# Cosine and sine tables of a Fourier mixer: split on the chip, or stored as high and low parts and fetched by GpSimd's queue

## The chip, the cores and the metric

One core of one Trainium2 chip runs the whole program. The metric is the device time of one execution in microseconds (us). The kernel before has a median of 1548.53 us over three runs (1547.23 to 1550.25).

## The reference, cut to what matters

The program is a two-layer transformer block on 512 image tokens and 256 context tokens of width 1024. Layer 0 mixes with Fourier transforms, layer 1 with attention. The change lies in layer 0's mixer, which runs for the image tokens (x) and for the context tokens (c):

```python
def _fourier_hyena_mixer(h, w_in, w_out, conv_w, conv_b, ...):
    proj = h @ w_in
    u_f = _f32(proj[..., :D_FOURIER]).reshape(B, L, N_FOURIER_GROUPS, FOURIER_GROUP_DIM)
    y_f = jnp.fft.fft2(u_f, axes=(1, 3), norm='ortho').real.reshape(B, L, D_FOURIER).astype(h.dtype)
    u_h = _dwconv3(proj[..., D_FOURIER:], conv_w, conv_b)
    x0, x1, v = jnp.split(u_h, 3, axis=-1)
    spectrum = _hyena_filter_spectrum(L, w1, b1, w2, b2, w3, b3, w4, freq)
    y_h = x0 * _long_conv(v * x1, spectrum, hy_bias)
    return jnp.concatenate([y_f, y_h], axis=-1) @ w_out
```

All of it is float32. The transforms are products with tables of cosines and sines, which depend on no input.

## The kernel before, in words

**Products in three parts.** A float32 matrix is kept as a high part and a low part, each in the matmul's own rounded format (F32R). A product is three matmuls, high by high, high by low and low by high (`mm3`, L266 to L269). To make the parts of a weight or a table, SyncE loads the raw float32 tile (`wraw`, L253, tile `wr`), ScalarE copies it into the rounded format (`hi`, L240 to L244, tile `wh`), and VectorE subtracts the copy from the raw tile (`lo`, L247, tile `wl`). The pool `W` holds three buffers each of `wr`, `wh` and `wl`, of 128 x 1024 float32 (512 KB) each. A buffer is free again when its last reader has finished.

**Order.** The steps of the mixer's second half stand in a written order, `MIX_ORDER`. It fixes the order among these steps on TensorE, VectorE, ScalarE and GpSimd, each of which takes its instructions in turn and stands still where one waits. The loads on SyncE's queue, and instructions of the code behind (the modulation sums `junk` of L368 and the splits of the first w_out tiles), are placed between them by the framework's scheduler.

**The steps**, by the names in `MIX_ORDER`; a digit at the end is the tile:
- R, WH, WL: load, high part and low part of a tile in `W`. The tiles are w_in 6 and 7, the four tables u0, u1 (`utab`) and i0, i1 (`itab`), and w_out 0 (o0). u0 and u1 take the long convolution to frequencies, i0 and i1 bring it back.
- P11, P60 to P63, P70 to P73: the last products with w_in. CA, CB, CC: their short convolution, on ScalarE and VectorE.
- HP: the pool of the normed input (hh, hl) is closed. Its memory goes to yh, yl and to the tables cs, ct and st: `cs128` (128 x 256), `fcos` (128 x 1040) and `fsin` (128 x 1024).
- TH and TL: high and low part of these three, in pieces c0, c1, n0, n1 and s0.
- FM, FD, T3, UH, UL: product, fold and transposition of the last piece of the convolution's input.
- SC, SX: to frequencies, context and image (tables u0 for SC0, SC1, SX0, SX1, and u1 for SX2, SX3). D, Q, Y, L with A or B: product with the filter's spectrum on VectorE (D), on GpSimd (Q), then high part (Y, ScalarE) and low part (L, VectorE for A, GpSimd for B).
- IC, IX: back from frequencies, context with i0, image with i0 and i1; E, S, M, H, L behind them: unfold, multiply by x0, split.
- FH, FL: parts of a Fourier group, in `W`. FA, GA: first transform with cs (image, context); PH, PL, GH, GL: parts of the result; FB, GB: second transform with ct and st; FE, FS, GE, GS: unfold. ZH, ZL: parts for the last product.
- OA, OB0 to OB3: the first tile of the product with w_out. The other seven follow in `res_proj`.

The products of P, SC, SX, FA, GA, FB, GB and O use three PSUM buffers in turn, IC and IX two others.

The loads and splits of the tables go through these lines:

```python
def wraw(self, src, n=1024):
    raw = self.t(self.W, [P, 1024], F32, "wr")
    self.nc.sync.dma_start(raw[:, :n], src)
    return raw
...
def TH(n):
    o, m = chunk(n)
    self.hi(k_[tabs[n[0]][2] + "h"][:, o : o + m], k_["raw" + n][:, :m])

def TL(n):
    (o, m), t_ = chunk(n), tabs[n[0]][2]
    self.lo(k_[t_ + "l"][:, o : o + m], k_["raw" + n][:, :m], k_[t_ + "h"][:, o : o + m])
```

Of the kernel before, what the change touches and what calls it, by code (L numbers as in the profile page):

```python
# [12 lines left out]
F32R = mybir.dt.float32r  # L13
# [7 lines left out]
P = 128  # L21
# [74 lines left out]
KAx3 G3 KBx3 SDAx2 RG4 SQx2 G4 SDAx0 SPBx2 KAx2 SPBx0 SDBx2 SQx0 KBx2 SDBx0  # L96
"""
MIX_ORDER = """
P11 R6 R7 WH6 WL6 P60 CA11 P61 CB11 CC11 P62 FM Ru0 WH7 FD T3 P63 WHu0 UH CA6 WL7 UL WLu0 CB6 SC0 Ru1 CC6 DBc0 SC1 DAc1 QBc0 YBc0 LBc0 WHu1 Ri0 Rn1
P70 QAc1 YAc1 WLu1 P71 DAc0 P72 QAc0 P73 YAc0 WHi0 SX0 LAc1 DBc1 HP QBc1 Rs0 LAc0 WLi0 SX1 CA7 YBc1 THn1 LBc1 CB7 DBx0 IC0 QBx0 DAx0 TLn1 IC1 QAx0 FH0  # L100
Rc0 THc0 ICE0 THs0 YBx0 ICE1 YAx0 Rn0 ICS0 CC7 LBx0 IC2 FL0 ICS1 TLs0 Rc1 IC3 THn0 LAx0 GA0 DAx1 DBx1 QAx1 SX2 GH0 QBx1 FA0 GL0 TLc0 THc1 YAx1 YBx1
LBx1 LAx1 FH1 TLn0 TLc1 DAx2 DBx2 SX3 PH0 GB0 ICM0 FH2 QAx2 QBx2 PL0 YAx2 ICH0 YBx2 LAx2 FL1 DAx3 GE0 ICE2 LBx2 DBx3 ICL0 FL2 FB0 FA1 FE0 GS0 PH1 QAx3
Ri1 GA1 QBx3 FS0 ICM1 PL1 YBx3 ICH1 FA2 WHi1 ICL1 ICE3 FB1 ICS2 LBx3 WLi1 GH1 YAx3 PH2 GL1 GA2 LAx3 Ro0 FE1 IX1 PL2 GB1 ICS3 ICM2 IXE1 IX0 IXS1 FH3
FS1 ICH2 ICM3 GH2 ICH3 ICL2 IXM1 IXH1 IXE0 ICL3 IX2 GE1 IXS0 FB2 FL3 GS1 IXE2 IXM0 GL2 FA3 FE2 IXH0 IXS2 IX3 IXM2 IXH2 FS2 GA3 PH3 IXL1 IXL0 PL3 IXL2
IXE3 IXS3 GB2 WHo0 IXM3 IXH3 FB3 GH3 GE2 FE3 WLo0 GL3 GB3 GE3 ZH0 IXL3 GS2 FS3 GS3 OA ZL0 OB0 ZH1 ZL1 ZH2 ZH3 OB1 ZL2 ZL3 OB2 OB3
"""


# [80 lines left out]
class Builder:  # L189
# [380 lines left out]
    def mixer(self):  # L570
        nc, I = self.nc, self.I
# [18 lines left out]
        x = [self.t(xp, [P, TW], F32, f"x{d}") for d in range(KD)]  # L590
        hh, hl = [], []
# [5 lines left out]
        with self.tc.manual_schedule(engines={ENG.PE, ENG.DVE, ENG.SP, ENG.Activation}):  # L597
# [30 lines left out]
            h = layer(0, layer(0, pa, 1), 2)  # L628
# [18 lines left out]
            def both(d, step):  # L647
                a1(d, step)
                return a2(d, step)
# [24 lines left out]
            h = layer(1, layer(1, pa, 1), 2)  # L674
# [45 lines left out]
        def conv(m, dst, ps):  # L720
            c = m - 4
            self.conv3(dst, ps, self.col("hcw0", c), self.col("hcw1", c), self.col("hcw2", c), self.col("hcb", c), TW)
# [230 lines left out]
        k_ = {}  # L953
        wt = {}
        pl = {}
        src = {"6": I["w_in"][6], "7": I["w_in"][7], "o0": I["w_out"][0], **{f"u{a}": I["utab"][a] for a in range(2)}, **{f"i{a}": I["itab"][a] for a in range(2)}}
        sx = lambda: self.t(pl["Sx"], [P, 512], F32, "sx")
        es = lambda: self.t(pl["Sx"], [P, 260], F32, "e", 4)
        tabs = {"s": ("cs128", 256, "cs"), "c": ("fcos", 1040, "ct"), "n": ("fsin", 1024, "st")}

        def R(n):
            if n in src:
                k_["raw" + n] = self.wraw(src[n])
            else:
                o, m = chunk(n)
                k_["raw" + n] = self.wraw(I[tabs[n[0]][0]][:, o : o + m], m)

        def chunk(n):
            o = 520 * int(n[1])
            return o, min(520, tabs[n[0]][1] - o)  # L970

        def WH(n):
            raw = k_["raw" + n]
            h, l = self.t(self.W, [P, 1024], F32R, "wh"), self.t(self.W, [P, 1024], F32R, "wl")
            self.hi(h, raw)
            wt[n] = h, l, raw

# [8 lines left out]
        def PP(m, q):  # L986
            if q == 0:
                k_[f"ps{m}"] = self.mm()
            for k in (2 * q, 2 * q + 1):
                self.proj_k(k_[f"ps{m}"], wt[str(m)], hh, hl, k)  # L990
# [53 lines left out]
        def SP(s, ft):  # L1044
            nt, kp, km = (1, 4, 5) if s == "c" else (2, 0, 2)
            th, tl, _ = wt[f"u{ft // 2}"]
            ps = k_[f"sp{s}{ft}"] = self.mm()
            even = ft < 2 if nt == 2 else ft == 0
            for c in range(2):
                k0 = kp if (c == 0) == even else km  # L1050
                for i in range(nt):
                    o = 512 * (ft % 2) + 256 * i + 128 * c
                    w = slice(o, o + 128)
                    self.mm3(ps[:, 512 * c : 512 * c + 512], th[:, w], tl[:, w], uTh[:, k0 + i, :], uTl[:, k0 + i, :], i == 0, i == nt - 1)
# [64 lines left out]


        def TH(n):
            o, m = chunk(n)
            self.hi(k_[tabs[n[0]][2] + "h"][:, o : o + m], k_["raw" + n][:, :m])

        def TL(n):
            (o, m), t_ = chunk(n), tabs[n[0]][2]
            self.lo(k_[t_ + "l"][:, o : o + m], k_["raw" + n][:, :m], k_[t_ + "h"][:, o : o + m])

        def FH(g):
            k_[f"fu{g}"] = [self.t(self.W, [P, 1024], F32R, t_)[:, :TW] for t_ in ("wh", "wl")]  # L1130
# [63 lines left out]
        def O(ks):  # L1194
            if 4 in ks:
                k_["o"] = self.mm()
            h, l, _ = wt["o0"]
            for k in ks:
                w = slice(128 * k, 128 * k + 128)
                self.mm3(k_["o"][:, 0:512], h[:, w], l[:, w], yh[k][:, 0:512], yl[k][:, 0:512], k == 4, k == 3)  # L1200

        def step(s):
            if s[0] == "R":
                R(s[1:])
            elif s[:2] in ("WH", "WL"):
                (WH if s[1] == "H" else WL)(s[2:])
            elif s in ("P11", "FM", "FD", "T3", "UH", "UL", "HP"):
                {"HP": HP, "P11": P11, "FM": FM, "FD": FD, "T3": T3, "UH": UH, "UL": UL}[s]()
            elif s[0] == "P" and s[1] in "67":
                PP(int(s[1]), int(s[2]))  # L1210
            elif s[0] == "C":
                conv(int(s[2:]), s[1])
            elif s[:2] in ("SC", "SX"):
                SP(s[1].lower(), int(s[2]))
            elif s[1] in "AB" and s[0] in "DQYL" and len(s) == 4:
                {"D": DD, "Q": QQ, "Y": YY, "L": LL}[s[0]]("AB".index(s[1]), s[2], int(s[3]))
            elif s[:2] in ("IC", "IX"):
                {"": inv, "E": IE, "S": IS, "M": IM, "H": IH, "L": IL}[s[2:-1]](s[1].lower(), int(s[-1]))
            elif s[:2] in ("TH", "TL"):
                (TH if s[1] == "H" else TL)(s[2:])  # L1220
            elif s in ("OA", "OB0", "OB1", "OB2", "OB3"):
                O(range(4, KD) if s == "OA" else [int(s[2])])
            elif s[0] == "Z":
                (ZH if s[1] == "H" else ZL)(int(s[2]))
            elif s[0] == "F" and s[1] in "HL":
                (FH if s[1] == "H" else FL)(int(s[2]))
            elif s[0] == "P":
                (F1H if s[1] == "H" else F1L)(0, int(s[2]))
            elif s[:2] in ("GH", "GL"):
                (F1H if s[1] == "H" else F1L)(4, int(s[2]))  # L1230
            else:
                {"A": F1, "B": F2, "E": F2E, "S": F2S}[s[1]](0 if s[0] == "F" else 4, int(s[2]))
# [1341 lines left out]
def _f(a):  # L2574
    return np.ascontiguousarray(a, dtype=np.float32)
# [5 lines left out]
    return o  # L2581


def constants():
    f32 = np.float32
    c = {}
# [32 lines left out]
    ut = np.zeros((4, P, 2, 2, P))  # L2619
    it = np.zeros((4, P, 2, C))  # L2620
# [5 lines left out]
        it[a, :, 0, :] = np.cos(ac).T  # L2626
        it[a, :, 1, :] = np.sin(asn).T
    it[0, 0] *= 0.5
    c["utab"] = ut.reshape(2, 2, P, 512).transpose(0, 2, 1, 3).reshape(2, P, 1024)
    c["itab"] = it.reshape(2, 2, P, 512).transpose(0, 2, 1, 3).reshape(2, P, 1024)  # L2630
    k = np.arange(258)
    ang = TWO_PI * ((t[:, None] * k[None, :]) % T) / T
    fc = np.zeros((T, 260))
    fc[:, :258] = np.cos(ang)
    c["fcos"] = fc.reshape(4, P, 260).transpose(1, 0, 2).reshape(P, 1040)
    sn = np.sin(ang[:, :256])
    c["fsin"] = sn.reshape(4, P, 256).transpose(1, 0, 2).reshape(P, 1024)
    m = np.arange(P)
    a8 = TWO_PI * ((m[:, None] * m[None, :]) % P) / P
    c["cs128"] = np.concatenate([np.cos(a8), np.sin(a8)], 1) / 256.0  # L2640
    rows, cols = np.repeat(np.arange(8), 64).astype(f32), np.tile(np.arange(64), 8).astype(f32)
    inv = (f32(10000.0) ** (-np.arange(8, dtype=f32) / f32(8))).astype(f32)
    co, si = np.zeros((32, T)), np.zeros((32, T))
# [103 lines left out]
def arrays_of(inputs):  # L2747
    a = layouts(**{k: np.asarray(v) for k, v in inputs.items()})
    a.update(constants())
    return {k: np.ascontiguousarray(v) for k, v in a.items()}  # L2750
# [16 lines left out]
```

## Time and profile before

| | |
|---|---|
| median of 3 runs | 1548.53 us (1547.23 to 1550.25) |
| profiled execution, its own time | 1556.88 us |
| span of its instructions | 1555.0 us |
| TensorE busy in the span | 1505.8 us, 97% |
| VectorE busy | 1262.1 us, 81% |
| ScalarE busy | 740.6 us, 48% |
| GpSimd busy | 250.8 us, 16% |
| loads of SyncE's and the hardware queue | 162.73 MB |
| loads of GpSimd's queue | 60.91 MB |

In the profile PE is TensorE, PEld its weight load, DVE VectorE, ACT ScalarE, POOL GpSimd, and SP SyncE; a q behind a name means the queue that only issues. "L247" is a line of the kernel, and since `hi`, `lo` and `mm3` are helpers, many tiles share their lines; one goes by the tile names. "out<-in" names what is written and what is read. A row of waits says who waited for what, for how long in total, how often, and the longest. Matmuls overlap, so TensorE's busy time is not time at its peak rate.

### The profile page before, as it was taken

The page shows a single profiled execution, that of the slowest core. Times are in us where ns is not written, and L with a number is a line of the kernel's source. Part 1 is how long each engine was busy: PE and PEld are TensorE (multiplying, and loading weights), DVE is VectorE, ACT ScalarE, POOL GpSimd, SP SyncE. Part 2 cuts the span into 40 slices and gives each one's busy share as a digit, 9 for nine tenths or more (in the row PEclk, how much of TensorE's full clock was granted, in tenths as well). Part 3 has the DMA queues.
Part 4 walks back from the last instruction along what each step waited for, and adds up shares of the span by engine and source line. Part 5 has one row for each costly group of instructions (what it writes and reads, how often), then busy time and mean ns, then how long its engine had stood idle before and what let it go on. Part 6 is the DMA issues. An engine that isn't in the chain of part 4 may idle for free.

```text
span 1555.0 us, 24353 instructions
## 1 busy us (share of the span) xinstructions
PE 1505.8 (97%) x9352; PEld 1308.7 (84%) x9352; DVE 1262.1 (81%) x2084; ACT 740.6 (48%) x1126; POOL 250.8 (16%) x406
## 2 busy tenths in 40 slices
PE   7999998999999999999999999999999899999998
PEld 5687887888999999989998888766558899989997
DVE  5788969968997998777768776889956899878884
ACT  4451224426544443434434345898844655434442
POOL 0013125201112121112111000111211121112100
PEclk9999999999999999999999999999999999999999
DMA  9336522546267779768687731010124465656543
GB/s 350 118 109 203 186 69 68 172 134 211 63 174 191 188 182 212 186 178 217 174 233 189 271 85 44 4 41 28 35 90 131 107 175 152 165 139 157 144 112 104
DMA packets 87872, 225.19 MB, mean 145 GB/s; under 512 B 12843, under 2 KB 19213, under 8 KB 86733
## 3 DMA queue, kind: packets, MB, share of 16 engines
q1 hardware_dynamic: 63565, 162.73, 31.5%
q0 software_dynamic: 24192, 60.91, 18.9%
q8 instruction: 73, 1.20, 0.3%
q14 instruction: 42, 0.34, 0.1%
HBM read 201.96 MB, written 21.64 MB: 144 GB/s over the span
## 4 chain that ended last, share of the span: by engine, by line
PE 66%; DVE 16%; DMA 9%; issue 4%; ACT 3%; POOL 1%; SPq 0%; ACTq 0%; POOLq 0%; DVEq 0%
PE mm L267 15%; PE mm L268 15%; PE mm L269 15%; DVE junk L368 4%; DMA sb<-wmodT 3%; DVE wl L247 3%; PE pv L2128 3%; PE ms L267 2%; PE ms L269 2%; DMA sb<-w_up 2%; PE ms L268 2%; PE s L2076 1%; DMA sa<-w_up 1%; PE pv L2139 1%; ACT wh L242 1%
## 5 line engine op out<-in xcount | busy, mean ns | idle before, releaser
L242 ACT ACTIVATE wh<-wr 128x1024 fp32r<-128x1024 f32 (+3 forms) x179 | 155.0, 875 | 200.2 <-PE mm L268 121.3
L267 PE MATMUL mm<-hh,wh 128*128 128x512 f32 (+3 forms) x704 | 231.5, 329 | 1.1 <-DVE xr L1370 1.0
L269 PE MATMUL mm<-hh,wl 128*128 128x512 f32 (+3 forms) x704 | 229.1, 325 | 3.4 <-DVE wl L247 3.3
L268 PE MATMUL mm<-hl,wh 128*128 128x512 f32 (+3 forms) x704 | 229.4, 326 | 2.3 <-DVE hl L450 2.3
L247 DVE TENSOR_TENSOR wl<-wr,wh 128x1024 fp32r<-128x1024 f32 (+3 forms) x179 | 180.5, 1013 | 19.3 <-ACT wh L242 18.4
L267 PEld LDWEIGHTS mm<-hh,wh 128*128 128x128 f32 x704 | 133.9, 190 | 13.2 <-issue 3.7
L269 PEld LDWEIGHTS mm<-hh,wl 128*128 128x128 f32 x704 | 133.4, 190 | 13.5 <-DVE wl L247 5.8
L268 PEld LDWEIGHTS mm<-hl,wh 128*128 128x128 f32 x704 | 133.8, 190 | 11.2 <-DVE hl L450 3.3
L368 DVE SCALAR_TENSOR_TENSOR junk<-wr,sb 128x1024 bf16<-128x1024 f32 x96 | 117.1, 1220 | 6.0 <-DMA wr<-wmodT 6.0
L267 PE MATMUL ms<-hh,wh 128*128 128x386 f32 (+2 forms) x240 | 76.2, 317 | 1.1 <-DVE fg L1554 0.9
L269 PE MATMUL ms<-hh,wl 128*128 128x386 f32 (+2 forms) x240 | 76.3, 318 | 0.0
L268 PE MATMUL ms<-hl,wh 128*128 128x386 f32 (+2 forms) x240 | 76.2, 317 | 0.0
L269 PE MATMUL mm<-x,wl 128*128 128x512 f32 (+1 forms) x224 | 75.8, 338 | 0.3 <-DVE wl L247 0.3
L267 PE MATMUL mm<-x,wh 128*128 128x512 f32 (+1 forms) x224 | 76.0, 340 | 0.0
L268 PE MATMUL mm<-x,wh 128*128 128x512 f32 (+1 forms) x224 | 76.0, 339 | 0.0
L267 PE MATMUL mm<-ah,wh 128*128 128x512 f32 x176 | 69.6, 396 | 0.0
L268 PE MATMUL mm<-al,wh 128*128 128x512 f32 x176 | 69.6, 396 | 0.0
L269 PE MATMUL mm<-ah,wl 128*128 128x512 f32 x176 | 69.6, 395 | 0.0
L2097 POOL PARTITION_ALL_REDUCE mx<-mx x16 | 34.0, 2130 | 199.3 <-DVE mx L2094 181.6
L2084 ACT ACTIVATE S<-s,rks 128x512 f32<-128x512 f32 x96 | 62.0, 694 | 5.8 <-PE s L2076 2.4
L2357 POOL DMA_DIRECT2D sum<-w_up x40 | 23.3, 590 | 237.5 <-DVE wl L247 161.9
L242 ACT ACTIVATE wh<-sum 128x1024 fp32r<-128x1024 f32 x40 | 42.3, 1059 | 37.3 <-PE mm L268 13.4
(539 smaller groups left out, 4480.7 us busy)
## 6 DMA issues: line engine op xcount, KB each, us to landing
wr<-wmodT SPq DMA_DIRECT2D x48, 512.0 KB
wr<-w_up SPq DMA_DIRECT2D x48, 512.0 KB
sum<-w_up POOLq DMA_DIRECT2D x80, 256.0 KB, 4.4
sb<-wmodT SPq DMA_DIRECT2D x32, 512.0 KB
xs<-delta POOLq DMA_DIRECT2D x32, 386.0 KB, 6.9
wr<-w_dn SPq DMA_DIRECT2D x48, 256.0 KB
sa<-w_up POOLq DMA_DIRECT2D x40, 256.0 KB, 4.3
sb<-w_up POOLq DMA_DIRECT2D x40, 256.0 KB, 5.2
```

Source lines behind the costliest of these rows:

```text
L242: self.nc.scalar.activation(dst, src, AF.Copy)
L247: (eng or self.nc.vector).tensor_tensor(dst, src, hi.bitcast(F32), op=ALU.subtract)
L267: mmul(out, wh, xh, start=start, stop=False)
L268: mmul(out, wh, xl, start=False, stop=False)
L269: mmul(out, wl, xh, start=False, stop=stop)
L368: nc.vector.scalar_tensor_tensor(junk, raw, 1.0, self.sb[j], op0=ALU.mult, op1=ALU.mult, accum_out=acc)
L2076: nc.tensor.matmul(ps, Kf[:, tok[j] : tok[j] + 128], q[0], start=True, stop=True)
L2084: nc.scalar.activation(c.S[a][:, j, :], c.ps[a, j], AF.Copy, scale=c.r[:, g : g + 1])
L2097: nc.gpsimd.partition_all_reduce(c.m[a][:, 1, :], c.m[a][:, 0, :], P, bass.bass_isa.ReduceOp.max)
L2128: nc.tensor.matmul(c.P[r : r + 32, :], V[:, j, 128 * p + r : 128 * p + r + 32], c.S[a][:, j, :], start=c.np == 0, stop=c.np == 5, tile_pos ...
L2139: nc.tensor.matmul(c.Z[o : o + 32, 0:256], ones, c.S[a][:, j, 256 * h : 256 * h + 256], start=c.nz == 0, stop=c.nz == 5, tile_position=(0, o))
L2357: nc.gpsimd.dma_start(t_[:, 512:1024], g[:, 0:512])
```

## The change

The tables are computed on the host in any case; now each is stored as two arrays, its high part and its low part, rounded as the matmul's format wants it (`_two`). The kernel loads both parts straight into the tiles `wh`, `wl` or `csh`, `csl` and so on, by GpSimd's queue, at the steps WHu0, WHu1, WHi0, WHi1 and THs0, THc0, THn0. The raw loads (Ru, Ri, Rs, Rc, Rn), the splits (WLu, WLi, TL) and their high copies are gone. The weights 6, 7 and o0 are loaded and split as before. `MIX_ORDER` is another order of the remaining steps, in which P70 to P73 stand ahead of P60 to P63. The arithmetic of every product is what it was.

```diff
-P11 R6 R7 WH6 WL6 P60 CA11 P61 CB11 CC11 P62 FM Ru0 WH7 FD T3 P63 WHu0 UH CA6 WL7 UL WLu0 CB6 SC0 Ru1 CC6 DBc0 SC1 DAc1 QBc0 YBc0 LBc0 WHu1 Ri0 Rn1
...
+P11 R6 WH6 WL6 R7 Ro0 WH7 WL7 P70 CA11 WHu0 CB11 P71 CC11 FM P72 FD P73 T3 CA7 WHi0 P60 UH CB7 UL P61 CC7 SC1 P62 DAc1 DBc1 QAc1 P63 HP QBc1 YAc1 LAc1
+SC0 CA6 THs0 FH1 CB6 THc0 YBc1 FL1 THn0 CC6 LBc1 DAc0 FA1 DBc0 QAc0 SX0 PH1 QBc0 YAc0 PL1 LAc0 YBc0 GA1 LBc0 DAx0 SX1 GH1 GL1 QAx0 DBx0 IC2 YAx0 FH0
+WHu1 IC3 LAx0 QBx0 ICE2 FL0 FB1 YBx0 ICS2 DAx1 ICE3 LBx0 ICS3 GB1 QAx1 FE1 DBx1 IC1 FS1 QBx1 GA0 IC0 ICM2 GH0 ICM3 ICH2 SX3 GL0 YAx1 ICL2 YBx1 LAx1 GE1
+LBx1 ICE1 GS1 ICH3 ICL3 FA0 DAx3 SX2 DBx3 FH2 QAx3 PH0 FL2 QBx3 YAx3 PL0 FA2 WHi1 YBx3 LAx3 FB0 LBx3 ICS1 ICE0 DAx2 DBx2 QAx2 PH2 ICS0 GB0 QBx2 ICM1
+YAx2 PL2 FE0 ICH1 YBx2 LAx2 FB2 LBx2 FS0 ICM0 ICL1 ICH0 GE0 ICL0 IX3 GS0 FE2 FS2 GA2 IXE3 IX0 IXS3 FH3 IXM3 GH2 FL3 IXH3 IX2 GL2 IXE0 IXL3 IXS0 IXM0
...
-        src = {"6": I["w_in"][6], "7": I["w_in"][7], "o0": I["w_out"][0], **{f"u{a}": I["utab"][a] for a in range(2)}, **{f"i{a}": I["itab"][a] for a in range(2)}}
+        src = {"6": I["w_in"][6], "7": I["w_in"][7], "o0": I["w_out"][0]}
+        two = {f"{n[0]}{a}": (I[n][0, a], I[n][1, a]) for n in ("utab", "itab") for a in range(2)}
...
         def WH(n):
+            h, l = self.t(self.W, [P, 1024], F32R, "wh"), self.t(self.W, [P, 1024], F32R, "wl")
+            if n in two:
+                for t_, s in zip((h, l), two[n]):
+                    nc.gpsimd.dma_start(t_, s)
+                wt[n] = h, l, None
+                return
             raw = k_["raw" + n]
-            h, l = self.t(self.W, [P, 1024], F32R, "wh"), self.t(self.W, [P, 1024], F32R, "wl")
             self.hi(h, raw)
...
         def TH(n):
-            o, m = chunk(n)
-            self.hi(k_[tabs[n[0]][2] + "h"][:, o : o + m], k_["raw" + n][:, :m])
-
-        def TL(n):
-            (o, m), t_ = chunk(n), tabs[n[0]][2]
-            self.lo(k_[t_ + "l"][:, o : o + m], k_["raw" + n][:, :m], k_[t_ + "h"][:, o : o + m])
+            tab, _, t_ = tabs[n]
+            for q, p in enumerate("hl"):
+                nc.gpsimd.dma_start(k_[t_ + p], I[tab][q])
...
+def _two(a):
+    def part(x):
+        u = x.view(np.uint32)
+        return ((u + 0x7FF + ((u >> 12) & 1)) & np.uint32(0xFFFFF000)).view(np.float32)
+
+    a = _f(a)
+    h = part(a)
+    return np.stack([h, part(a - h)])
...
-    c["utab"] = ut.reshape(2, 2, P, 512).transpose(0, 2, 1, 3).reshape(2, P, 1024)
+    c["utab"] = _two(ut.reshape(2, 2, P, 512).transpose(0, 2, 1, 3).reshape(2, P, 1024))
```

`itab`, `fcos`, `fsin` and `cs128` are stored by `_two` in the same way.

More of the change, by code (lines that the diff above doesn't have):

```diff
@@ L98 @@
 MIX_ORDER = """
-P11 R6 R7 WH6 WL6 P60 CA11 P61 CB11 CC11 P62 FM Ru0 WH7 FD T3 P63 WHu0 UH CA6 WL7 UL WLu0 CB6 SC0 Ru1 CC6 DBc0 SC1 DAc1 QBc0 YBc0 LBc0 WHu1 Ri0 Rn1
[L100 to L105, printed above, removed]
+P11 R6 WH6 WL6 R7 Ro0 WH7 WL7 P70 CA11 WHu0 CB11 P71 CC11 FM P72 FD P73 T3 CA7 WHi0 P60 UH CB7 UL P61 CC7 SC1 P62 DAc1 DBc1 QAc1 P63 HP QBc1 YAc1 LAc1
[3 more added lines that the diff above has]
+YAx2 PL2 FE0 ICH1 YBx2 LAx2 FB2 LBx2 FS0 ICM0 ICL1 ICH0 GE0 ICL0 IX3 GS0 FE2 FS2 GA2 IXE3 IX0 IXS3 FH3 IXM3 GH2 FL3 IXH3 IX2 GL2 IXE0 IXL3 IXS0 IXM0
+FA3 IXE2 IXH0 IXS2 IX1 IXL0 PH3 IXM2 PL3 IXH2 IXL2 GB2 IXE1 WHo0 IXS1 GA3 GE2 FB3 IXM1 GH3 GS2 IXH1 GL3 WLo0 GB3 FE3 IXL1 FS3 ZH1 OA ZH2 ZL1 ZH0 ZL2
+GE3 ZL0 OB1 GS3 OB2 OB0 ZH3 ZL3 OB3
 """
@@ L961, in R @@
         def R(n):
-            if n in src:
-                k_["raw" + n] = self.wraw(src[n])
-            else:
-                o, m = chunk(n)
[L966 to L970, printed above, removed]
-        def WH(n):
+            k_["raw" + n] = self.wraw(src[n])
+        def WH(n):
+            h, l = self.t(self.W, [P, 1024], F32R, "wh"), self.t(self.W, [P, 1024], F32R, "wl")
[4 more added lines that the diff above has]
+                return
             raw = k_["raw" + n]
-            h, l = self.t(self.W, [P, 1024], F32R, "wh"), self.t(self.W, [P, 1024], F32R, "wl")
             self.hi(h, raw)
@@ L1121, in TH @@
         def TH(n):
-            o, m = chunk(n)
-            self.hi(k_[tabs[n[0]][2] + "h"][:, o : o + m], k_["raw" + n][:, :m])
-        def TL(n):
-            (o, m), t_ = chunk(n), tabs[n[0]][2]
-            self.lo(k_[t_ + "l"][:, o : o + m], k_["raw" + n][:, :m], k_[t_ + "h"][:, o : o + m])
+            tab, _, t_ = tabs[n]
+            for q, p in enumerate("hl"):
+                nc.gpsimd.dma_start(k_[t_ + p], I[tab][q])
         def FH(g):
@@ L1218, in step @@
                 {"": inv, "E": IE, "S": IS, "M": IM, "H": IH, "L": IL}[s[2:-1]](s[1].lower(), int(s[-1]))
-            elif s[:2] in ("TH", "TL"):
-                (TH if s[1] == "H" else TL)(s[2:])
+            elif s[:2] == "TH":
+                TH(s[2])
             elif s in ("OA", "OB0", "OB1", "OB2", "OB3"):
@@ L2628, in constants @@
     it[0, 0] *= 0.5
-    c["utab"] = ut.reshape(2, 2, P, 512).transpose(0, 2, 1, 3).reshape(2, P, 1024)
-    c["itab"] = it.reshape(2, 2, P, 512).transpose(0, 2, 1, 3).reshape(2, P, 1024)
+    c["utab"] = _two(ut.reshape(2, 2, P, 512).transpose(0, 2, 1, 3).reshape(2, P, 1024))
+    c["itab"] = _two(it.reshape(2, 2, P, 512).transpose(0, 2, 1, 3).reshape(2, P, 1024))
     k = np.arange(258)
@@ L2634, in constants @@
     fc[:, :258] = np.cos(ang)
-    c["fcos"] = fc.reshape(4, P, 260).transpose(1, 0, 2).reshape(P, 1040)
+    c["fcos"] = _two(fc.reshape(4, P, 260).transpose(1, 0, 2).reshape(P, 1040))
     sn = np.sin(ang[:, :256])
-    c["fsin"] = sn.reshape(4, P, 256).transpose(1, 0, 2).reshape(P, 1024)
+    c["fsin"] = _two(sn.reshape(4, P, 256).transpose(1, 0, 2).reshape(P, 1024))
     m = np.arange(P)
     a8 = TWO_PI * ((m[:, None] * m[None, :]) % P) / P
-    c["cs128"] = np.concatenate([np.cos(a8), np.sin(a8)], 1) / 256.0
+    c["cs128"] = _two(np.concatenate([np.cos(a8), np.sin(a8)], 1) / 256.0)
     rows, cols = np.repeat(np.arange(8), 64).astype(f32), np.tile(np.arange(64), 8).astype(f32)
```

## The prediction

> **What bounds the kernel now.** I read the totals first, then the busy time by stretch, then what TensorE waits for, then the chain of waits.
>
> ```profile
> span 1555.0 us, 24353 instructions
> ```
>
> The change touches one stage only, the mixer's second half. The view of busy time by stretch cuts it into four. The columns are the busy time and, in brackets, the instructions of each engine, then the granted TensorE clock, the DMA share and GB/s.
>
> ```profile
> core 0: us, PE busy (x) PEld busy (x) DVE busy (x) ACT busy (x) POOL busy (x), PEclk, DMA share, GB/s
> 212.60:240.00 27.40, 26.95 (x146) 22.75 (x145) 21.45 (x26) 11.23 (x14) 11.89 (x26) 1.00 0.12 36
> 240.00:252.00 12.00, 9.01 (x52) 8.59 (x52) 10.30 (x19) 4.02 (x10) 6.80 (x7) 0.72 0.20 62
> 252.00:296.00 44.00, 41.04 (x316) 38.90 (x314) 43.01 (x82) 22.63 (x42) 15.16 (x33) 1.00 0.34 107
> 296.00:307.00 11.00, 9.40 (x40) 7.79 (x41) 10.93 (x24) 3.49 (x7) 4.63 (x43) 0.84 0.73 253
> sum 94.40, PE 86.39 PEld 78.03 DVE 85.69 ACT 41.37 POOL 38.48; mean PE 21.60 PEld 19.51 DVE 21.42 ACT 10.34 POOL 9.62
> ```
>
> The stage runs from the first matmul of P60 at 212.6 us to the end of OB3 near 307.0. From 240 on VectorE is busy 64.2 of 67.0 us (10.30 + 43.01 + 10.93), so it is the engine that others wait for. TensorE loses 94.4 - 86.4 = 8.0 us idle. In two stretches its clock is below full: 9.01 x 0.28 = 2.5 us and 9.40 x 0.16 = 1.5 us, together 4.0. What is left, 82.4 us, is TensorE's own work at full clock. So **12.0 us** is all that this stage can give while the matmuls stay the same. The waits of TensorE in it (total, times, longest):
>
> ```profile
> PE ms L267 <- DVE e L1105: 3.0, 2, 1.7
> PE mm L267 <- DVE pql L1157: 2.5, 2, 2.1
> PE mm L267 <- ACT pqh L242: 1.2, 1, 1.2
> PE mm L267 <- DVE sx L1062: 0.7, 1, 0.7
> PE mm L269 <- DVE wl L247: 0.5, 1, 0.5
> ```
>
> Nearly all end on VectorE. The largest single one stands in the chain of waits; three splits of w_out (3.5 us, row below under the sum) stand on VectorE just ahead of it, and only one of them (WLo0) is in the written order.
>
> ```profile
> 293.45 1.77 DVE wl L247 x2
> ...
> 297.60 0.37 PE mm L267
> ```
>
> **Removed: the splits of the tables.** Groups of VectorE, then of ScalarE (count | busy us, mean ns | idle before):
>
> ```profile
> L247 DVE TENSOR_TENSOR wl<-wr,wh 128x1024 fp32r<-128x1024 f32 x4 | 6.2, 1553 | 1.9 <-ACT wh L242 1.9
> L247 DVE TENSOR_TENSOR stl<-wr,sth 128x504 fp32r<-128x504 f32 (+1 forms) x2 | 2.6, 1282 | 0.0
> L247 DVE TENSOR_TENSOR ctl<-wr,cth 128x520 fp32r<-128x520 f32 x2 | 1.4, 687 | 0.0
> L247 DVE TENSOR_TENSOR csl<-wr,csh 128x256 fp32r<-128x256 f32 x1 | 0.4, 412 | 0.0
> ```
>
> ```profile
> L242 ACT ACTIVATE wh<-wr 128x1024 fp32r<-128x1024 f32 x5 | 5.1, 1045 | 0.0
> L242 ACT ACTIVATE cth<-wr 128x520 fp32r<-128x520 f32 x2 | 1.3, 636 | 1.1 <-DMA wr<-fcos 1.1
> L242 ACT ACTIVATE sth<-wr 128x504 fp32r<-128x504 f32 (+1 forms) x2 | 1.2, 624 | 0.8 <-DMA wr<-fsin 0.8
> ```
>
> The four wl are u0, u1, i0, i1 (the window holds no other). VectorE loses 6.2 + 2.6 + 1.4 + 0.4 = 10.6 us, in the stretch where it is full, and 75.1 of 85.7 stay. That is below TensorE's 82.4, so TensorE becomes the bound. ScalarE loses four of the five wh, 4 x 1.05, and some 2.9 for the smaller tables, 7.1 us, and gains nothing by it: it is busy 41.4 of 94.4. SyncE loses nine loads, and their raw buffers go to later weights. R6, R7 and Ro0 now stand at the head, so Ro0 keeps one of three raw buffers for the whole stage; two are left to turn over.
>
> **Added: fourteen loads on GpSimd's queue**, high and low part of seven tables, twice the bytes (some 6.6 MB for 3.3). Loads that GpSimd issues now, with KB each and median us to landing; then one line's issues with ns on GpSimd (least, median, most); then a 512 KB load that SyncE issued, as the chain shows it:
>
> ```profile
> x<-xT POOLq DMA_DIRECT2D x8, 256.0 KB, 3.3
> x<-cxT POOLq DMA_DIRECT2D x8, 128.0 KB, 3.0
> xs<-delta POOLq DMA_DIRECT2D x32, 386.0 KB, 6.9
> ```
>
> ```profile
> L1302 POOL DMA_DIRECT2D x<-cxT x8: 536/537/862, 260.1 to 307.4; - x8
> ```
>
> ```profile
> 192.15 3.40 DMA wr<-w_in
> ```
>
> Issues: 14 x 0.54 = 7.5 us, at most 14 x 0.86 = 12.0. GpSimd is busy 38.5 of 94.4, so this is hidden; its cover would be gone only where the queue itself waits. The landing of a pair of 512 KB is not in the trace. Lower end, at SyncE's rate: 0.54 + 2 x 3.40 = 7.3 us. Upper end, two of the slowest row: 2 x 6.9 = 13.8, or 18.3 if that row is also scaled to 512 KB. I take 7.3: the 256 KB row takes only 0.3 us more than the 128 KB one, so bytes are cheap here, and the stage uses 0.12 to 0.34 of the DMA engines until 296.
>
> The row first: of eight issues one took 0.86 us and the median 0.54. [...]
>
> **Waits that the new order adds.** A load into a wh/wl buffer must wait until TensorE has left it, and GpSimd stands still meanwhile. Cover is counted in matmuls, from two runs of matmuls without a gap (first and last of 12, first and last of 24):
>
> ```profile
> 255.56 0.40 PE L267 MATMUL mm<-uTh,wh 128*128 128x512 f32 x1
> ...
> 258.13 0.40 PE L269 MATMUL mm<-uTh,wl 128*128 128x512 f32 x1
> ...
> 273.47 0.28 PE L267 MATMUL ms<-wh,s 128*128 128x256 f32 x1
> ...
> 276.18 0.28 PE L269 MATMUL ms<-wh,s 128*128 128x256 f32 x1
> ```
>
> So 0.234 us each at 512 columns (2.57/11), 0.118 at 256 (2.71/23). A column costs the same in both; 772 columns are 0.35.
>
> - u0 waits for P11. Behind it stands FM, which needs CC11 anyway, 3 us later. TensorE has P7, half of P6 before SC1: 36 x 0.35 = 12.6 us against 7.3. Hidden.
> - i0 waits for P73 and is first read at IC2, over 20 us on. Hidden.
> - cs, cos and sin wait for P63, the last reader of hh. Only SC0 lies between P63 and FA1: 6 x 0.234 = 1.4 us. The pair of 128 KB takes 0.54 + 3.0, so **FA1 waits 2.1 us**. If QBc1 ahead of the issue is late as well, another 1.5:
>
> ```profile
> L1069 POOL TENSOR_TENSOR sx<-sx,sx 128x512 f32<-128x512 f32 x12 | 17.5, 1467 | 11.0 <-DVE sx L1062 7.2 <-DVE sx L1064 3.6
> ```
>
> - u1 waits for SX1, with QBx0 and LBx0 behind it. Until SX3 TensorE has four IC, FB1, GB1 and GA0: 48 + 24 + 12 + 6 = 90 matmuls at 0.118, 10.6 us against 7.3. Hidden.
> - i1 waits for SX2, with LBx3 behind it. Until IX3 reads it: FA2, FB0, GB0, FB2 and six of IX3, 78 x 0.118 = 9.2 us against 7.3. Hidden by 1.9.
>
> **The sum.** Of the present waits, 3.0 (e) and 0.5 (wl) stood behind splits that are gone. The other 4.5 can stay or go; I keep 1.0, near the low end, since VectorE falls from 91% to 75.1/87 = 86% of the stage. Waits afterwards: 2.1 + 1.0 = 3.1, bounds 0 and 2.1 + 1.5 + 4.5 = 8.1. The clock: the stretch with a 2.1 us wait lost 1.5, the one with 1.7 and 1.3 lost 2.5. One wait of 2.1 is like the former, so 1.5, bounds 0 and 4.0. Gain: 12.0 - 3.1 - 1.5 = **7.4 us**. The stage would take 87.0 us.
>
> The trace: a clock of 0.84 and 0.72 in the stretches with waits of 2.1 and 1.7. [...]
>
> Nothing after the stage takes the gain back as I see it:
>
> ```profile
> 300.00:360.00 60.00, 60.00 (x314) 51.22 (x314) 45.84 (x91) 20.72 (x31) 6.27 (x19) 0.98 0.49 164
> L368 DVE SCALAR_TENSOR_TENSOR junk<-wr,sb 128x1024 bf16<-128x1024 f32 x7 | 8.5, 1217 | 0.9 <-DMA wr<-wmodT 0.9
> L247 DVE TENSOR_TENSOR wl<-wr,wh 128x1024 fp32r<-128x1024 f32 x3 | 3.5, 1221 | 0.0
> ```
>
> The next product keeps TensorE full with VectorE at 45.8 of 60, so VectorE has 14.2 us free for whatever of the seven modulation sums (8.5 us, laid into this stage by the scheduler, not by the written order) no longer fits. The profiled execution took 1556.88 us, 1.88 around its span; it would take 1549.5. The median of the runs is 8.35 below it, and the same 7.4 gives **1541.1**.
>
> **Rivals.**
> - *All of it* (0.13): the loads land inside SC0 and the clock holds. Nothing in the rows lands in 1.4 us, but an earlier issue is possible. 12.0 us, 1536.5.
> - *VectorE stays full* (0.14): freed raw buffers let the scheduler lay more modulation sums and w_out splits into the stage, as it did with 8.5 and 3.5 us. For: 293.45 above. Against: it can only take what it believes to be idle. Waits 4.5 + 2.1, clock 4.0: gain 1.4, 1547.1.
> - *Late pairs; slower* (0.13): a pair takes 13.8 us. Late: u0 by 1.2, u1 by 3.2, i1 by 4.6, together 9.0; with 3.1 and clock 4.0 that is 16.1 against 12.0: 4.1 slower, 1552.6. It decides from lateness 12.0 - 7.1 = 4.9, a pair of 12.4 us ((12.4 - 10.6) + (12.4 - 9.2) = 5.0). For: 6.9 us on this queue. Against: that row writes while much else moves.
> - *It does not shorten the kernel* (0.08): the stage ends earlier, but the next product waits for its weights, each needing a wh/wl buffer that i0, i1 or o0 holds to the end. For: 253 GB/s at 296 to 307, the highest of the stage. 1548.5.
>
> **How the numbers follow.** The forecast has 0.52; its own range is 1538.5 to 1545.0. A measurement of this kernel tells no change from one within 0.2%, 3.1 us. Faster: 0.50 of the forecast, 0.13, and 0.07 from the better half of *full* and *not shorter*: 0.70. Slower: 0.13. Same: 0.17. The range goes down past *all of it* and up to halfway between no change and *late pairs*: 1535 to 1550.
>
> **What would show it.** In the profile after, no wl, ctl, stl or csl split on VectorE in the stage, and fourteen table loads on GpSimd's queue. VectorE some 10.6 us lighter; TensorE idle 3 us instead of 8, its longest wait at the first csh matmul, and one dip of the clock. It would be wrong if TensorE waited at the first u1 matmul of SX3 or the i1 matmul of IX3 for a load, if LBc1 or QBx0 on GpSimd came late behind a waiting load, or if the modulation sums filled VectorE again.

## The result and the profile after

The changed kernel takes 1543.66 us (median of 20 runs, 1537.74 to 1553.96), beside 1551.68 us for the kernel before on the same chip (20 runs). The ratio is 0.9945, 95% interval 0.9926 to 0.9964, which is 8.5 us of 1551.7 with an interval of 5.6 to 11.5. The forecast was a gain of 7.4 us. The total came near it, but only in part for the reason given: the stage gave less than forecast, and a part of the gain that nobody forecast lies far behind it. The ratios below are each to the kernel before, run beside the kernel in question.

The span of the profiled execution, from the head of the page:

```profile
span 1536.0 us, 24330 instructions
```

The stage in the view of busy time by stretch (busy us and instructions of PE, PEld, DVE, ACT and POOL, then the granted clock, the DMA share and GB/s). It now runs from the first matmul of P70 at 212.9 us to the end of OB3 at 303.1 us:

```profile
core 0: us, PE busy (x) PEld busy (x) DVE busy (x) ACT busy (x) POOL busy (x), PEclk, DMA share, GB/s
212.90:240.00 27.10, 24.44 (x131) 21.07 (x130) 17.05 (x26) 6.26 (x8) 13.84 (x37) 0.94 0.48 159
240.00:268.00 28.00, 28.00 (x196) 25.88 (x196) 24.74 (x46) 11.15 (x23) 20.87 (x19) 1.00 0.34 110
268.00:290.00 22.00, 20.92 (x167) 20.72 (x167) 16.09 (x33) 10.43 (x20) 4.76 (x7) 0.92 0.17 50
290.00:303.10 13.10, 12.17 (x68) 9.83 (x68) 11.89 (x22) 6.11 (x12) 5.96 (x62) 1.00 0.58 200
sum 90.20, PE 85.53 PEld 77.51 DVE 69.78 ACT 33.95 POOL 45.43; mean PE 21.38 PEld 19.38 DVE 17.44 ACT 8.49 POOL 11.36
```

The stage takes 90.2 us, 4.2 less than 94.4, where the forecast had 87.0. VectorE is no longer full: it is busy 69.8 of 90.2 us, where it was 85.7 of 94.4. TensorE is idle 90.20 - 85.53 = 4.67 us, where it was 8.0. The clock is below full in two stretches. What TensorE waited for, in the stage and the thirteen microseconds ahead of it (total, times, longest):

```profile
PE mm L267 <- DMA csh<-cs: 2.7, 1, 2.7
PE mm L929 <- DVE tm L922: 2.6, 1, 2.6
PE mm L267 <- DVE pql L247: 1.1, 1, 1.1
PE mm L268 <- DVE yl L247: 0.9, 1, 0.9
```

The splits of tables are gone from VectorE. Of the wl out of raw buffers three are left in the stage, all of w_out, as in before; from the view of groups of VectorE:

```profile
L247 DVE TENSOR_TENSOR wl<-wr,wh 128x1024 fp32r<-128x1024 f32 x3 | 3.6, 1217 | 0.0
```

The loads that took the place of the table splits, from the view of transfers (KB each, median us from issue to landing):

```profile
wh<-utab POOLq DMA_DIRECT2D x2, 512.0 KB, 4.5
wl<-utab POOLq DMA_DIRECT2D x2, 512.0 KB, 5.6
wh<-itab POOLq DMA_DIRECT2D x2, 512.0 KB, 3.8
wl<-itab POOLq DMA_DIRECT2D x2, 512.0 KB, 4.5
csh<-cs POOLq DMA_DIRECT2D x1, 128.0 KB, 2.3
```

Two dips of the clock stand in the stage. The same view of busy time, cut finely to them:

```profile
236.20:239.60 3.40, 3.40 (x14) 3.05 (x15) 2.88 (x5) 0.24 (x1) 3.34 (x6) 0.50 1.07 352
...
270.30:273.70 3.40, 3.40 (x18) 3.40 (x17) 2.87 (x10) 0.57 (x2) 1.92 (x2) 0.51 0.21 64
```

Each dip is 3.4 us at half clock, so 1.7 us lost, and each begins shortly behind a wait: TensorE resumes at 236.15 and 269.99, and the clock falls at 236.2 and 270.3.

**How the lengths are compared below.** A runs from the last fold of the convolution's input on GpSimd (L917) to the first addition of the product with w_out. B has the same start and ends at the norm behind that product (L408). The tail is all behind that norm. Idle is the time in which no matmul runs, and clock is half the time at half clock, both from the trace. The rest is matmul work at full clock.

| kernel (profile) | A | B | idle in B | clock in B | rest of B | tail |
|---|---|---|---|---|---|---|
| before, 1st | 106.3 | 177.8 | 12.5 | 5.1 | 160.2 | 1176.4 |
| before, 2nd | 106.1 | 176.4 | 11.3 | 5.1 | 159.9 | 1166.9 |
| before, 3rd | 106.4 | 177.0 | 11.7 | 5.1 | 160.2 | 1177.7 |
| before, 4th | 106.7 | 177.0 | 10.7 | 6.8 | 159.5 | 1172.4 |
| after, 1st | 103.5 | 172.6 | 9.8 | 3.4 | 159.4 | 1163.5 |
| after, 2nd | 103.3 | 172.3 | 9.7 | 3.4 | 159.1 | 1164.1 |
| after, 3rd | 103.5 | 172.5 | 9.8 | 3.4 | 159.3 | 1165.5 |
| after, 4th | 103.7 | 172.6 | 10.3 | 3.4 | 159.0 | 1164.6 |

By the means of four profiles each, B became shorter by 177.05 - 172.5 = 4.5 us: 1.7 idle, 2.1 clock, 0.7 rest. A alone gave 2.9; the other 1.6 lie between the first addition and the norm. A also holds some 12 us ahead of the stage, which became 1.2 us longer; the stage itself, from P60 or P70 to the end of OB3, takes 94.3 to 95.0 us in the profiles of before and 90.2 to 90.6 in those of after. The tail became shorter by 1173.3 - 1164.4 = 8.9 us. The profiled spans of before are on average 13.7 us longer than those of after, more than the 8.5 us of the timed runs, so the tail's share in a mean run is nearer 4 us by estimate (8.5 - 4.5).

### The profile page after: what moved, and what is told of

Its sections match the earlier page's. It is cut to its first block, busy times and chain, and to the rows that moved or that the text cites. A ratio compares the mean times of both kernels' runs of the same rounds, so it can differ in the third digit from the quotient of the medians.

```text
span 1536.0 us, 24330 instructions
## 1 busy us (share of the span) xinstructions
PE 1498.9 (98%) x9352; PEld 1305.0 (85%) x9352; DVE 1251.7 (81%) x2075; ACT 735.4 (48%) x1117; POOL 258.4 (17%) x420
## 4 chain that ended last, share of the span: by engine, by line
PE 77%; DVE 12%; DMA 6%; ACT 2%; issue 2%; POOL 1%; SPq 0%; ACTq 0%; DVEq 0%; POOLq 0%
PE mm L267 18%; PE mm L268 18%; PE mm L269 18%; DMA sb<-wmodT 3%; PE ms L267 3%; PE ms L268 3%; PE ms L269 3%; DVE junk L368 3%; PE pv L2123 3%; DVE wl L247 3%; PE s L2071 1%; PE pv L2134 1%; PE s L267 1%; PE s L268 1%; PE s L269 1%
## 5 line engine op out<-in xcount | busy, mean ns | idle before, releaser
L242 ACT ACTIVATE wh<-wr 128x1024 fp32r<-128x1024 f32 (+3 forms) x175 | 151.0, 872 | 199.2 <-PE mm L268 109.5
L247 DVE TENSOR_TENSOR wl<-wr,wh 128x1024 fp32r<-128x1024 f32 (+3 forms) x175 | 174.4, 1001 | 14.7 <-ACT wh L242 14.1
L268 PEld LDWEIGHTS mm<-hl,wh 128*128 128x128 f32 x704 | 134.5, 191 | 11.3 <-DVE hl L450 3.3
L368 DVE SCALAR_TENSOR_TENSOR junk<-wr,sb 128x1024 bf16<-128x1024 f32 x96 | 117.1, 1220 | 6.1 <-DMA wr<-wmodT 5.9
```

The lines of the kernel that those rows point to most:

```text
L242: self.nc.scalar.activation(dst, src, AF.Copy)
L247: (eng or self.nc.vector).tensor_tensor(dst, src, hi.bitcast(F32), op=ALU.subtract)
L268: mmul(out, wh, xl, start=False, stop=False)
L368: nc.vector.scalar_tensor_tensor(junk, raw, 1.0, self.sb[j], op0=ALU.mult, op1=ALU.mult, accum_out=acc)
```

## The experiments

**The changed kernel once more.**

> The changed kernel once more, to see which parts of the gain repeat. Two lengths are read from each profile: A, from the GpSimd product of the last folded piece (L917) to the first sum with the w_out product (before 106.3 us, after 103.5 in the first profiles), and B, from the same start to the second norm's sum nrm_s (before 177.8, after 172.6). Theory 1, the stage gives the gain: A 103.5 and B 172.6 again, within 1 us, and the 13 us by which the two first profiles differ behind the norm are changes of the clock that fall otherwise in each execution. Theory 2, the gain lies behind the stage: the later parts are shorter again by 10 us or more.

Ratio 0.9939 (0.9916 to 0.9963), A 103.3, B 172.3. A and B repeat within 0.4 us in the four profiles of after, and within 0.6 and 1.4 us in those of before. The other kernels have one profile each, in which one dip more or less is 1.7 us.

**The tables in parts, but the old order.** The order of before, with the steps struck that no longer exist:

```diff
-P11 R6 R7 WH6 WL6 P60 CA11 P61 CB11 CC11 P62 FM Ru0 WH7 FD T3 P63 WHu0 UH CA6 WL7 UL WLu0 CB6 SC0 Ru1 CC6 ...
+P11 R6 R7 WH6 WL6 P60 CA11 P61 CB11 CC11 P62 FM WH7 FD T3 P63 WHu0 UH CA6 WL7 UL CB6 SC0 CC6 ...
```

> The tables as high and low parts by GpSimd's queue, in the old order with the removed steps struck out (each table at the place of its first piece). Theory 1, VectorE's lost 10.6 us are the gain and the order fits it to the loads: some loads come late, since the old order has SX2 soon after FH1 and FH0, but A is still under 106.3, about 105; ratio about 0.997. Theory 2, the order is the gain: A 106 or more, ratio 1.000 or above.

Ratio 0.9991 (0.9973 to 1.0009): no change in the total. A is 111.8, 5.5 longer than before, with 11.8 us idle and 8.5 of clock, and B is 182.2, 5.1 longer than the mean of before. The tail, 1164.3, is as short as in after: this kernel loses in and around the stage what it gains far behind it. Its waits of TensorE from 200 to 312 us:

```profile
PE mm L267 <- DVE x L1008: 3.1, 1, 3.1
PE mm L929 <- DVE tm L922: 2.5, 1, 2.5
...
PE mm L267 <- DMA csh<-cs: 0.9, 1, 0.9
PE mm L269 <- DMA wl<-utab: 0.8, 1, 0.8
PE mm L267 <- DMA wh<-utab: 0.4, 1, 0.4
```

In the old order the tables land too late in three places (2.1 us together), and the convolution (L1008) is late for 3.1 us. Taking 10.6 us off VectorE makes the stage longer, not shorter, in an order that was laid out around that work.

**The new order, but raw tables that are split on the chip.** The new order, with the loads and splits of before put in ahead of their readers:

```diff
-WHu0 CB11 P71 CC11 FM P72 ... WHu1 IC3 ... WHi1 YBx3 ...
+Ru0 ... WHu0 Ri0 CB11 P71 CC11 WLu0 FM P72 ... WHu1 WLu1 Ri1 IC3 ... WHi1 WLi1 Ro0 YBx3 ...
```

> The new order with the tables loaded raw by SyncE and split on the chip as before (the raw loads and the splits are put in by hand close to the steps that they feed). Theory 1: VectorE has its 10.6 us back and stands in front of TensorE in several places; A at least 106, more likely 108 to 112, ratio 1.000 to 1.006. Theory 2, the order is the gain: A 103 to 104, ratio 0.995.

Ratio 1.0024 (1.0007 to 1.0041): slightly slower than before. A 110.5, B 179.7 (2.6 longer than the mean of before), tail 1169.5. The waits of TensorE are on VectorE again:

```profile
PE mm L267 <- DVE sx L1062: 3.5, 2, 2.4
...
PE ms L267 <- DVE e L1105: 1.1, 1, 1.1
```

So neither half alone carries the gain in B. The order needs the lighter VectorE, and the lighter VectorE needs the order.

**SX0 ahead of FA1.**

```diff
-SC0 CA6 THs0 ... FA1 DBc0 QAc0 SX0 PH1 ...
+SC0 SX0 CA6 THs0 ... FA1 DBc0 QAc0 PH1 ...
```

> The changed kernel with one step moved: SX0 stands ahead of FA1, so that TensorE has 2.8 us of work while the cosine and sine tables cs land. Theory 1, the wait of 2.7 us at FA1 and the dip of the clock behind it are on the path: both vanish, A 103.5 - 2.7 - up to 1.6, 99.5 to 101, ratio about 0.992. Rival, VectorE's chain behind DAc0 sets the end in any case: the wait vanishes but TensorE waits as long a little later, A 103 to 104, ratio 0.995.

Ratio 0.9924 (0.9901 to 0.9947). A is 99.9, 3.6 shorter than after (103.5). The waits of TensorE are now:

```profile
PE mm L929 <- DVE tm L922: 2.5, 1, 2.5
PE mm L267 <- DVE sx L1062: 1.6, 1, 1.6
PE mm L267 <- DVE pql L247: 1.2, 2, 1.1
PE mm L268 <- DVE yl L247: 0.9, 1, 0.9
```

The wait for csh is gone, and A has no dip at all: 7.3 us idle and 3.4 of clock became 6.2 and 0, with 1.0 us of matmul work more in A. The clock gave more than the wait. The length is the one that theory 1 named, but not by its terms: of the 2.7 us of wait, 1.6 come back a little later (sx L1062), which is part of what the rival said, and two dips went instead of one. B is 170.3, only 2.2 shorter than in after, since one dip of 1.7 stands behind A, at 368.7 us. The timed runs do not tell this kernel from after (0.9939, 0.9916 to 0.9963, measured beside it).

**The modulation sums kept out of the stage.** In after, four instructions of the modulation sums (L368) start between 201.9 and 212.9 us; in before there are none between 197 and 273. The timeline of VectorE in after shows the first of them in front of the fold (start, us, line, ..., idle before and what ended it):

```profile
201.90 1.23 DVE L368 SCALAR_TENSOR_TENSOR junk<-wr,sb 128x1024 bf16<-128x1024 f32 x1 [2.11 <-DMA wr<-wmodT]
203.05 0.08 DVE L368 DVE_READ_ACCUMULATOR junk<-wr,sb 128x1 f32 x1
203.05 0.42 DVE L922 TENSOR_TENSOR tm<-tm 128x256 f32<-128x256 f32 x1
```

VectorE waits 2.11 us for the raw weight of the sum, and the fold stands behind it, so the transposition (L929) waits 2.6 us on TensorE. In before this wait was shorter:

```profile
203.25 0.98 PE L929 MATMUL mm<-cst,tm 128*128 128x128 f32 x6 [1.32 <-DVE tm L922]
```

The edit issues these sums behind the last split (yl) of the mixer:

```diff
                 if len(gl) > 8:
-                    self.gemv_dve(*gl.pop(0))
+                    with self.tc.issue_after(self.mix_end):
+                        self.gemv_dve(*gl.pop(0))
```

> The changed kernel, but each modulation sum that the scheduler lays into the mixer's second half is issued only behind the mixer's last split (yl); nothing is left out. Theory 1 (two sums that moved ahead of the stage hold the fold on VectorE, whence the transposition at L929 waits 2.65 instead of 1.32 us; in the stage they only use idle time): that wait falls to 1.3 to 1.5, A by 0 to 1.5 (102 to 103.5), and the sums reappear behind the stage, where VectorE has room, so B stays at 171 to 173. Rival (the sums do no harm where they are, and behind the stage they take room that the next product needs): A 103.3 as before, B 174 to 178, time 3 to 6 us up. Time by theory 1: 0.992 to 0.995 of the kernel before.

Ratio 0.9918 (0.9897 to 0.9940), A 102.1, B 171.6. The waits:

```profile
PE mm L267 <- DVE x L1008: 2.6, 1, 2.6
PE mm L929 <- DVE tm L922: 1.3, 1, 1.3
PE mm L267 <- DVE pql L247: 1.1, 1, 1.1
PE mm L267 <- ACT yh L242: 1.0, 1, 1.0
PE mm L268 <- DMA csl<-cs: 0.2, 1, 0.2
```

The transposition's wait is back at 1.3, A is 1.2 to 1.6 shorter and B 0.7 to 1.0, so the following product does not take it back. The tail of this profile is 1167.5, 2 to 4 longer than in after (idle 17.0, clock 6.8, beside 14.6 to 16.8 and 3.4 to 5.7); the timed runs show no loss.

**What FA1 waits for.** Without the sums FA1's wait is as long as in after, but that view puts it down to the convolution's last step (L1008). Its first matmul awaits several events, and the view names the one that came last. In after these two end together:

```profile
232.47 1.29 POOL L1067 TENSOR_TENSOR sx<-sx,sx 128x512 f32<-128x512 f32 x1
233.70 0.57 POOL L1122 DMA_DIRECT2D csh<-cs  x1
```

```profile
234.97 1.02 DVE L1008 SCALAR_TENSOR_TENSOR x<-mm,pcol,x 128x771 f32<-128x771 f32 x1
```

```profile
236.15 0.50 PE L267 MATMUL mm<-csh,wh 128*128 128x256 f32 x1 [2.66 <-DMA csh<-cs]
```

The load lands 2.3 us after its issue, at 236.0, and the convolution ends at 234.97 + 1.02 = 236.0. These times do not say which of the two FA1 needs. The new order with raw tables does: there FA1 starts 1.1 us before the same step (L1010 in that kernel) begins.

```profile
233.93 0.39 PE L267 MATMUL mm<-csh,wh 128*128 128x256 f32 x1 [0.73 <-ACT wh L242]
```

```profile
235.01 1.02 DVE L1010 SCALAR_TENSOR_TENSOR x<-mm,pcol,x 128x771 f32<-128x771 f32 x1
```

The program of after says the same. The PSUM buffers do not go strictly in turn: FA1 gets the one of SC1, and what its first matmul awaits of VectorE is the last reading of SC1's product (L1060), done at 230.4. So in after FA1 waits for the load, and the load is late because its issue stands behind QBc1 (1.29 us, L1067) on GpSimd. By estimate a faster load would have saved about 1 us, until FA1's third matmul waited for the low part wl, which VectorE finishes at 235.05.

**Both edits.**

> Both edits: SX0 ahead of FA1, so that the load of the tables cs lands under 36 matmuls more, and the modulation sums behind the mixer's last split. Theory 1: the two waits are at different places and add: no wait for csh, the transposition's wait 1.3 to 1.5, A 98.5 to 100, B 168.5 to 170.5, 0.990 to 0.993 of the kernel before. Rival (the sums behind the stage take it back): A 99.9, B 172 or more, 0.994 or above.

Ratio 0.9913 (0.9889 to 0.9937), A 100.0, B 169.4. B is 7.7 shorter than before's mean. A gained nothing over SX0 alone: 1.0 us less idle, but one dip (1.7) in A, where the other has it behind A. The tail of this profile is 1169.2, 4 to 6 longer than in after. Its time, 1537.33 beside 1549.87 for before, is the lowest here, though the intervals of the three last kernels overlap with each other and with that of after.

**The load of i1 issued just ahead of its reader.**

```diff
-... PL0 FA2 WHi1 YBx3 ... GE0 ICL0 IX3 ...
+... PL0 FA2 YBx3 ... GE0 ICL0 WHi1 IX3 ...
```

> The changed kernel with one step moved: the loads of the table i1 are issued just ahead of IX3, its first reader, instead of behind FA2, some 9 us later. Nothing is left out. Theory 1 (a pair of 512 KB costs about 6 us to landing, and only the matmuls under it hide it): the issue moves from 263.6 to about 272.8, landing at 277 to 279, TensorE reads i1 at about 276, so a wait of 1 to 3.5 us at wh or wl of L267/L268 appears, perhaps with one dip of the clock of 1.5: A 104.5 to 108. Rival (a pair is slow in the stage, 12 to 14 us, as my prediction's late case had it; the short landings seen were lucky): a wait of 9 to 11 us, A 113 to 116. Second rival (cover plays no part, the scheduler starts the load where it likes): no wait, A 103.4.

Ratio 0.9962 (0.9942 to 0.9982), A 106.8, 3.3 longer than after, as theory 1 had it; 2.8 of it are the two new waits. GpSimd's timeline and the two waits of TensorE:

```profile
271.94 0.55 POOL L969 DMA_DIRECT2D wh<-itab  x1
```

```profile
276.14 0.36 PE L267 MATMUL ms<-wh,s 128*128 128x256 f32 x1 [1.99 <-DMA wh<-itab]
277.33 0.51 PE L268 MATMUL ms<-wl,s 128*128 128x256 f32 x1 [0.83 <-DMA wl<-itab]
```

From the first issue to the first reading of the second part it is 277.33 - 271.94 = 5.4 us. That is the price of a pair when nothing covers it, and 12 us or more, as the case of late pairs needed, is excluded here.

**More profiles of both kernels.** The difference of the first two profiles in the tail was large (13 us), so both kernels were profiled again.

> The kernel before, once more, for a second profile of it. Three lengths are compared: A, from the last fold of the convolution's input (L917 on GpSimd) to the first addition of the product with w_out; B, from the same start to the following norm (L408); and the tail behind that norm. Before: A 106.3, B 177.8, tail 1176.4 us. After, in four kernels with tables in parts: tail 1163.2 to 1164.3. Theory 1 (the gain lies in the stage, and the tail of the first profile was one unlucky execution, with clock dips at other places): A 106 and B 178 again within 0.5, tail 1164 to 1168, span 1543 to 1547. Rival (about half of the difference of the two profiles lies behind the stage, in what the scheduler lays there): tail 1174 to 1178 again. The ratio to the kernel before should be 1.000 within 0.002 by both.

> A third profile of the kernel before, to split the gain between the stage and what lies behind. Theory 1 (4 to 5 us of the gain lie between the last fold and the norm, the rest in a wait of 1.5 us for the weights of the second product with T3h, near 768 us, and in single dips of the clock of 1.7 us that fall by chance): B 176 to 178, the T3h waits there again (0.87 and 0.64), tail 1165 to 1176. Rival (the tail has nothing of the gain): no T3h wait, tail 1163 to 1165 as after.

> A third profile of the changed kernel. Theory 1: B 172 to 173, two dips in the stage, no T3h wait, tail 1162 to 1167. Rival (the tail has nothing of the gain, first profiles were chance): T3h wait in some of them, tail spread as widely as before's, 1163 to 1176.

> A fourth profile of the kernel before; the same numbers as for the third: B 176 to 178 and the T3h waits by theory 1, and a tail whose length follows the number of dips, 1.7 us each.

> A fourth profile of the changed kernel; the same numbers as for the third: B 172 to 173, no T3h wait by theory 1, and a tail whose length follows the number of dips, 1.7 us each.

The second run of the kernel before has a ratio of 1.001 (0.999 to 1.003) and a tail of 1166.9, which looked as if the first had been unlucky. The third and fourth have 1177.7 and 1172.4. All four tails of after lie within 1163.5 to 1165.5. So the tail does hold a part of the gain, and the expectation of a tail that is chance alone fell. Single profiles of the other kernels spread more: 1163.2 to 1169.2 with tables in parts, 1169.5 with raw tables in the new order. The matmul work in it is the same within 1.6 us (1143.1 to 1144.7 in all eight); what differs is idle time and dips. Much of it lies in one place, the products with the tile T3h, whose weights come from w_up. Waits of TensorE from 620 to 790 us and what ScalarE waited for, of before (third profile), then of after (third):

```profile
PE mm L267 <- DVE fv L1551: 3.9, 2, 3.4
PE mm L267 <- ACT wh L242: 1.7, 1, 1.7
PE mm L269 <- DVE wl L247: 1.5, 2, 0.8
...
ACT wh L242 <- DMA sb<-w_up: 14.1, 3, 5.7
```

```profile
PE mm L269 <- DVE wl L247: 0.8, 1, 0.8
...
ACT wh L242 <- DMA sb<-w_up: 2.9, 1, 2.9
```

Summed over the T3h matmuls, TensorE is idle 4.4, 1.9, 6.3 and 3.5 us in the four profiles of before, and 0.0, 0.1, 0.0 and 1.2 in those of after. Before has one to two dips there (1.7 or 3.4 us), after none. By the means that is 4.0 + 2.6 - 0.3, some 6 of the 8.9 us. In one profile each it goes with the form of the tables and not with the order: the new order with raw tables has 3.2 us and a dip there, the old order with tables in parts 0.5 and none. The four other kernels with tables in parts have 0.1 to 2.2, where before's least is 1.9, and none has a dip there.

How the tables reach so far is open. SyncE issues the same loads in the same order behind the norm in both kernels, and loads of w_up by GpSimd's queue land after similar times (median 4.2 to 5.4 us in both). Where the inputs lie in memory may differ, since the tables are twice as large; that was not tried.

## Why the prediction was right, and where not

- **The total.** 7.4 us forecast, 8.5 (5.6 to 11.5) measured. In the stage itself it was too high: 4.2 us came (4.3 by the means of four profiles), and B, which ends at the norm, gave 4.5. The statement that the change touches one stage only fails; the T3h product gave some 6 us in these profiles, and the tail some 4 us in a mean run. That this fills the total up to the forecast is luck.
- **Removed and added work.** As forecast. VectorE fell from 85.7 to 69.8 us: 10.6 for the splits, and most of the other 5.3 for instructions of the modulation sums (seven, 8.5 us, in the stage before, three, 3.7 us, after). ScalarE fell by 7.4 (7.1 forecast), GpSimd rose by 7.0 (7.5 forecast). Its issues took 0.54 to 0.59 us, but one 0.86 (the first, at 213.29); why is not shown.
- **The price of a pair.** 7.3 taken, 0.55 + 5.6 = 6.2 us at the median of u, and 5.4 measured bare with i1. The covers for u0, u1 and i1 held: after has no wait for them, and the wait came at once when i1's cover was taken away. The case of late pairs is out.
- **FA1.** The wait came at the named matmul, 2.66 instead of 2.1 us. The mechanism is the one forecast, but two errors made the number: the pair landed in 2.9 us and not 3.5 (issue at 233.70, csl at 236.6), and the issue stood behind QBc1 for 1.29 us, which the forecast named as a case (1.5) and left out of its sum.
- **Other waits.** Mis-sized: 1.0 kept, 2.0 measured (pql 1.1, yl 0.9). With FA1 this is 4.67 instead of 3.1, so idle time in the stage fell by 3.3 and not by 4.9.
- **The clock.** Mis-sized twice. The loss before was 5.1 us, not 4.0: busy time times the lack of clock misses the part of a dip in which the window counts idle. Afterwards I took one dip of 1.5, and there were two, 3.4 together. The gain was 1.7 (2.1 by the means) and not 2.5.
- **A step that was missing.** The sums move. The rival *VectorE stays full* saw that the scheduler could lay more of them into the stage; it laid two ahead of it, one of them in front of the fold, and the transposition waited 1.3 us longer. Undoing it shortened A by that much.
- **The rivals.** *All of it* (12.0 us in the stage) did not come, but the two edits above bring B to 7.7 us below before. *It does not shorten the kernel* is out: the following product did not take the gain back, and B is shorter by more than A.

Taken over A, the terms close: idle 9.1 to 7.4 and clock 5.5 to 3.4 are 3.8 us of gain, and 0.9 more matmul work in A (91.8 to 92.7) leaves 2.9. The forecast took the matmuls of the stage as unchanged. In fact eight matmuls of the second tile of w_out stand ahead of OB3's last one, where before has three (557 matmuls from 212.9 to 303.1 us and 552 from 212.5 to 307.1, each taken as one window); these five, 5 x 0.234 = 1.2 us, are then missing behind the first addition, where the rest fell from 68.2 to 66.5. The other 0.5 us of that has no cause shown.

## What to carry to other kernels

Removing work from the busiest engine paid here only together with an order that is laid out for what is left; each half alone made A and B longer (A 111.8 and 110.5, beside 106.1 to 106.7 before). When a load and a computation end together ahead of a wait, the times alone do not say which of them it needs: look at the program, or at a run in which the two come apart. Extend the window of the forecast beyond the stage on both sides: work that a scheduler places freely moves across its border.

## What the runs showed of the hardware

In the traces of before and after the granted clock is either full or half, and the stretches at half clock are 3.413 us, or 6.827, two times that (the last one, which the end of the run cuts off, aside). A dip thus costs 1.7 us or a multiple, and the clock lost in B is 5.1 or 6.8 us in the four profiles of before and 3.4 in those of after. In after, a wait of 2.66 us and one of 1.08 us were followed by one:

```profile
269.99 0.39 PE L267 MATMUL mm<-cth,pqh 128*128 128x258 f32 x1 [1.08 <-DVE pql L247]
```

In the kernel with SX0 first, a wait of 1.6 us and one of 1.1 us were not: the clock is 1.00 from 212.6 to 301.8 us. Nor is a wait needed: in before a dip begins at 951.4 us (clock 0.50 until 958.2), behind 11.4 us, from 940.0 on, in which some matmul was running all the time.

Within each of the two traces the starts of all dips lie whole multiples of 3.413 us apart; the two in after, at 236.2 and 270.3, are ten apart. If one cuts after's trace at these multiples, FA1's wait of 2.66 us lies in one stretch (232.8 to 236.2), and a dip follows; the transposition's, as long, is cut at 202.07 into 1.10 and 1.55 us, and none follows. But the stretch ahead of 270.3 has only 1.08 us idle, and a dip follows it too, so the idle time of a stretch does not decide alone, and what does is open.
